# A two-layer hybrid backbone: elementwise work of the RWKV and LRU stage taken off GpSimd, and a quota on the products issued beside it

## The chip, the cores and the metric

The kernel runs on one core of a Trainium2 chip. The metric is device time in microseconds (us), the median of repeated runs. The engines are named as in the profile: PE is TensorE (PEld its weight loads), DVE is VectorE, ACT is ScalarE, POOL is GpSimd, SP is SyncE, which here issues most DMAs.

## The reference, cut to what matters

256 latent and 256 context tokens of width 1024 pass through two layers. Each layer is a half-step SwiGLU, three parallel mixers on one input projection, gated merge and output projection, and a second half-step SwiGLU. In the second layer the context tokens only feed the latent ones.

```python
z = _modulate(x, norm_g[l, 1], m[3], m[4]) @ w_in[l]          # and zc for the context tokens
ya = windowed attention(za); yl = _lru_mixer(zl, ...); yr = _rwkv_mixer(zr, ...)
# LRU, each of 2 directions: a = exp(log_a); b = sqrt(-expm1(2 log_a)) * (i * u); scan h = a h + b
# RWKV, each of 2 directions and 8 heads of 64, token by token:
sa = einsum('bhvk,bhk->bhv', s, -kk_t)
s  = s * w_t + sa * (kk_t * a_t) + v_t * k_t                  # outer products over v, k
o  = einsum('bhvk,bhk->bhv', s, r_t)
out = (g0 * (ya @ proj[0]) + g1 * (yl @ proj[1]) + g2 * (yr @ proj[2])) @ w_o   # g = sigmoid(zg)
```

## The kernel before, in words

All large matrices are multiplied in three products of a high and a low part (hi x hi, hi x lo, lo x hi). `wload` (L191 to L216) fetches a weight tile by a DMA on SP's queue, copies it to its high part on ACT (L206) and takes the difference as its low part on DVE (L215). Here the profile's phases matter: in the phases `r0` and `r1` (`POOL_PART`, L35) a quarter of the columns, 256 of 1024, is taken by POOL (L214) and DVE takes 768.

The stage that the change touches runs once per layer, between attention and the merge. It holds the LRU mixer (`lru`), the RWKV mixer (`rwkv`) and, beside them, the projections that depend on neither: 32 tiles of 24 products each, 768 products, in the generator `tiles` (8 tiles `x`, `u` feed the LRU, 24 are the gates). In the first layer a product is 512 columns wide; in the second one only the four `x` tiles are, the others are 256 wide. After the step `switch` two of the three branch projections join the queue, 192 products more.

The order of the instructions in this stage is fixed by a planner, `Weave`, when the program is built. Each mixer is split into generators (`first`, `second`, `setup`, `head`, `direction`, `pairs`, `bonus`, `decay`, `invert`, `values`, `recur`, `last`), and each `yield step(...)` announces what the next instructions will cost PE, DVE, ACT and POOL and what they need. `run` keeps a planned time `t`; it takes the step of the lowest priority number that is ready, and it issues a product instead where no step is ready, where the step at hand has PE work and the planned PE activity of the last stretch is `low`, or where an LRU tile is wanted. So the planner issues products as soon as it has a use for them, until there are none.

The RWKV recurrence is done in chunks of 64 tokens for two heads at a time (f = 0 to 3). Per f: `head` and `direction` prepare decays and keys, `pairs` multiplies them, `invert` solves a triangular system by 28 small DVE instructions between block transposes (L1160 to L1172), `invert_rest` finishes it with small matmuls (`pq`, `pw`, `pz`), `values` and `recur` carry the state (`pu`, `pM`, `po`). In the LRU, L870, L893 and L906 are POOL multiplies and adds; in RWKV POOL does L1049, L1087, L1098 and the multiply of `decay`, L1133. With DVE they form chains: ACT's tanh, POOL's product, DVE's product, and so on.

Of the kernel before, what the change touches and what calls it, by code (L numbers as in the profile page):

```python
# [26 lines left out]
NCH = T // CH  # L27
HOP, BACKLOG, WINDOW, ACTIVE, PERIOD = 0.25, 1.5, 3.4, 3.3, 50.0
E05 = float(np.exp(np.float32(-0.5)))
# [4 lines left out]
POOL_LO = {'z0': 1, 'z1': 1}  # L34
POOL_PART = {'r0': 0.25, 'r1': 0.25}  # L35
FIRST_AT = {5: [2], 6: [3, 0], 7: [1, 4]}
# [59 lines left out]
def build(tc, a, out, upto=99, dbg=None):  # L96
# [3 lines left out]
    with es:  # L100
# [472 lines left out]
        def seg3(ap):  # L573
            return ap.rearrange("p (s t) -> p s t", s=2)
# [152 lines left out]
        def step(pe=0.0, area=0.0, dve=0.0, act=0.0, pool=0.0, lag=1, need=()):  # L727


            return pe, area, (dve, act, pool), lag, need  # L730

        class Weave:
# [12 lines left out]

            def products(self):
                if not self.fill(1):
                    return False
                self.busy(*self.product)
                return True  # L750
# [7 lines left out]
            def run(self, *parts):  # L758

                at = [[b, g, None, []] for b, g in parts]  # L760
                for p in at:
                    self.advance(p, 0.0)
                while at:
                    best, soonest, wanted = None, 1e9, False
                    for p in at:
                        pe, area, eng, lag, need = p[2]
                        if any(k not in self.done for k in need):
                            wanted |= any(k[0] in "xu" for k in need)
                            continue
                        ready = p[3][-lag] if 0 < lag <= len(p[3]) else 0.0  # L770
                        ready = max([ready] + [f - BACKLOG for f, e in zip(self.free, eng) if e] + [self.done[k] for k in need])
                        soonest = min(soonest, ready)
                        if ready <= self.t and (best is None or p[0] < best[0]):
                            best = p
                    low = sum(b for a, b in self.recent if a > self.t - WINDOW) < ACTIVE
                    if best is None or (low and best[2][0]) or (wanted and self.t > self.owed):
                        if self.products():
                            self.owed = self.t + self.product[0]
                            continue
                        if best is None:  # L780
                            self.t = soonest
                            continue
                    pe, area, eng, lag, need = best[2]
                    self.busy(pe, area)
                    end = self.t
                    for i, e in enumerate(eng):
                        if e:
                            self.free[i] = max(self.free[i], self.t + HOP) + e
                            end = max(end, self.free[i] + HOP)
                    best[3].append(end)  # L790
                    best[0] += max(pe, *eng)
                    self.advance(best, end)
                    if best[2] is None:
                        at.remove(best)

            owed = 0.0

# [3 lines left out]
        def lru(l, yd, done):  # L801
# [8 lines left out]
            def first(set_):  # L810
# [30 lines left out]
                for f in range(4):  # L841
# [3 lines left out]
                    gl = lp.tile([P, T], F32, tag="gl", name=f"gl{l}{f}")  # L845
                    yield step(dve=2.1, act=0.65, need=[("x", f)] + [("scanned", f - 2)] * (f > 1))
                    ps = tile_of["x", f]
# [9 lines left out]
                    for d in range(2):  # L857
# [9 lines left out]
                        c = slice(d * 4 + f, d * 4 + f + 1)  # L867
                        yield step(dve=0.7, act=1.95, pool=1.6)
                        nc.scalar.activation(tg[1], tg[1], AF.Identity, bias=one)
                        nc.gpsimd.tensor_tensor(bb[:, d], tg[1], xc, ALU.mult)  # L870
                        nc.scalar.activation(aa[:, d], tg[0], AF.Exp, bias=n4[:, c], scale=n4[:, c])
                        nc.scalar.activation(th[:, d], tg[0], AF.Tanh, bias=n2[:, c], scale=n2[:, c])
                        nc.vector.scalar_tensor_tensor(bb[:, d], aa[:, d], 1.0, bb[:, d], ALU.add, ALU.mult)
                    yield step(dve=1.4, act=1.3, pool=0.7, need=[("u", f)])
                    ps = tile_of["u", f]
                    read[0] += 1
                    u, w, o = ps[:, qc:], gl[:, qc:], lp.tile([P, T], F32, tag="gu", name=f"gu{l}{f}", bufs=1)
                    nc.scalar.square(w, u)
                    nc.gpsimd.tensor_scalar(w, w, 0.044715, 1.0, ALU.mult, ALU.add)
                    nc.vector.tensor_tensor(w, w, u, ALU.mult)  # L880
# [5 lines left out]
            def second(set_):  # L886
                for f in range(4):
# [3 lines left out]
                    for d in range(2):  # L891
                        yield step(pool=1.6, lag=1 - d)
                        nc.gpsimd.tensor_tensor(bb[:, d], th[:, d], bb[:, d], ALU.mult)  # L893
                    for d in range(2):
                        yield step(dve=1.3, lag=2)
                        A, B, H = aa[:, d], bb[:, d], th[:, d]
                        if d == 0:
                            nc.vector.tensor_tensor_scan(H, A, B, 0.0, ALU.mult, ALU.add)
                        else:
# [3 lines left out]
                                                         H[:, 0:1], ALU.mult, ALU.add)  # L903
                    yield step(dve=0.7, pool=1.6)
                    y = lp.tile([P, T], F32, tag="yl", name=f"yl{l}{f}", bufs=1)
                    nc.gpsimd.tensor_tensor(y[:, qc:], th[:, 0, qc:], th[:, 1, qc:], ALU.add)  # L906
                    nc.vector.scalar_tensor_tensor(y[:, qc:], y[:, qc:], 0.25, gl[:, qc:], ALU.mult, ALU.mult)
# [39 lines left out]
        def step_view(ap, d):  # L947
            v = seg3(ap)
            return v if d == 0 else v[:, :, ::-1]

        def rwkv(l, rk, z, zd, yd, weave, beside, before_last):
# [7 lines left out]
            with ExitStack() as ey:  # L959
# [3 lines left out]
                wup, aup = (rx.tile([P, T], F32, tag=n, name=f"{n}{l}") for n in ("wup", "aup"))  # L963
                hv = rx.tile([P, 28], F32, tag="hv28", name=f"hv{l}")
                st, Y = {}, {}

                def setup():
# [6 lines left out]
                    nc.vector.tensor_scalar(hv[:, 20:24], V[:, R_KA:R_KA + 4], 0.5, None, ALU.mult)  # L974
                    nc.vector.tensor_scalar(hv[:, 24:28], hv[:, 20:24], -1.0, 1.0, ALU.mult, ALU.add)
                    nc.scalar.activation(twd, twd, AF.Tanh)
                    nc.scalar.activation(sgd[:, qc:], sgd[:, qc:], AF.Tanh, scale=0.5)
# [3 lines left out]
                    for f in range(4):  # L981
# [4 lines left out]
                        head_rows(pss, sq, f, 0, lambda q: f == 0, f == 3)  # L986
                    yield step(dve=4.5, act=0.4)
                    st["rsK"] = head_rsqrt(rx, rt, "tw0", pss, 0, 1.0, 1e-24, ALU.max, f"k{l}")
# [54 lines left out]
                def direction(f, d):  # L1043
                    nm = f"{l}{f}"

                    yield step(dve=1.22, pool=0.62, lag=0, need=[("tw", f)])
                    ar, bt, pc, kk, bon, tws, tas = st[f]
                    tw = tws[d]
                    nc.gpsimd.tensor_scalar(tw, tw, -0.5 * E05, -0.5 * E05, ALU.mult, ALU.add)  # L1049
                    twj = tw.rearrange("p (j t) -> p j t", t=CH)  # L1050
# [17 lines left out]
                    nc.vector.tensor_tensor(bt[:, 0, d, :, 1], ta.rearrange("p (j t) -> p j t", t=CH), iP, ALU.mult)  # L1068
                    yield step(dve=1.4, pool=1.6 * d, lag=0, need=[("one", f)] * d + [("loaded", f)] * (f > 1))
                    kks = step_view(kk, d).rearrange("p s (j t) -> p s j t", t=CH)  # L1070
# [10 lines left out]
                    if d == 0:  # L1081

                        bon.append(km)
                        weave.set("one", f)
                    else:
                        bon = bon[0]
                        nc.gpsimd.tensor_tensor(seg3(bon)[:, s0:], seg3(bon)[:, s0:], step_view(km, 1)[:, s0:], ALU.add)  # L1087
                        weave.set("both", f)
# [3 lines left out]
                def bonus(f):  # L1092

                    nm = f"{l}{f}"
                    yield step(dve=0.75, pool=1.15, lag=0, need=[("both", f)])
                    bon = st[f][4][0]

                    nc.gpsimd.tensor_copy(seg3(k_[f]), step_view(v_[f], 1))  # L1098
                    weave.set("values", f)
# [27 lines left out]
                def decay(f, d):  # L1127

                    nm = f"{l}{f}"
                    yield step(pool=1.9, lag=0, need=[("paired", f, d)])  # L1130
                    bt, pc = st[f][1:3]
                    bkT = bt[:, 0].rearrange("p d j h c -> p d j (h c)")
                    nc.gpsimd.tensor_tensor(bkT[:, d], bkT[:, d], pc[:, d, :, None].to_broadcast([P, NCH, P]), ALU.mult)  # L1133
                    for j4 in range(2):
# [248 lines left out]
                def finish(fs, pool):  # L1383

                    yield step(dve=4.5, act=0.4)
                    rsO = head_rsqrt(pool, pool, "hvo", Y["oss"], qc // P, 1.0 / 64, 64e-5, ALU.add, f"o{l}{fs[0]}")
# [257 lines left out]
```

## Time and profile before

| | |
|---|---|
| median of 3 runs | 2797.81 us (2794.79 to 2802.01) |
| the profiled execution | 2800.25 us |
| its span, first to last instruction | 2798.4 us |
| mean granted PE clock | 0.940 |
| PE, DVE, ACT, POOL busy | 94%, 62%, 38%, 15% of the span |

The stage described above lies from about 611 to 1062 us for the first layer and from about 2105 to 2560 us for the second. Busy time is the union of an engine's instructions. The granted clock is the mean over a stretch of the two levels, 1.2 GHz (0.5) and 2.4 GHz (1.0), so 0.75 means that half the stretch was at the lower one. A wait is put down to the instruction that came last. "issue" is time in which an engine waited for nothing that the profile shows.

### The profile page before, as it was taken

Reading aid. Unit: us, or ns where it says so; the run is one execution under the profiler, and the core shown is the slowest. Engines: PE = TensorE matmul, PEld = TensorE weight load, DVE = VectorE, ACT = ScalarE, POOL = GpSimd, SP = SyncE. Lnnn points to the kernel's source line nnn. Section 1 sums busy time; section 2 is a strip of 40 time slices with the busy share of each in tenths; the row PEclk is TensorE's granted clock in tenths of the full one; section 3 lists DMA queues with packets and bytes.
Section 4 is the critical chain, followed back from the end, with each engine's and each line's share of the span. In section 5 each row is a group of like instructions: output and inputs, shape, how many; then the busy total and the mean of one; then the engine's idle time right before and its main releaser. Section 6 shows DMA issues by size and latency. Waiting matters only on the chain. (4 is left out here: it accounts for less than half of the span.)

```text
span 2798.4 us, 47830 instructions
## 1 busy us (share of the span) xinstructions
PE 2629.1 (94%) x19761; PEld 2186.4 (78%) x19761; DVE 1730.3 (62%) x2934; ACT 1058.6 (38%) x1673; POOL 406.7 (15%) x381
## 2 busy tenths in 40 slices
PE   7999999997999999899999999999998899887899
PEld 5788888765677776798888978888776788777899
DVE  5867557657666644766655674555657656646565
ACT  4323233335544432332323432324346544333343
POOL 1000002224311102300000100001134432113000
PEclk9999999998898979999999999999999897768999
DMA  7646433122221125735443464544224331026465
GB/s 268 211 151 188 139 98 110 57 80 68 65 65 41 52 82 181 243 91 151 145 119 97 153 194 155 170 153 119 74 78 126 86 90 53 4 78 179 125 184 159
DMA packets 480092, 341.85 MB, mean 122 GB/s; under 512 B 17307, under 2 KB 448884, under 8 KB 479618
## 3 DMA queue, kind: packets, MB, share of 16 engines
q1 hardware_dynamic: 460690, 314.22, 37.2%
q10 hardware_dynamic: 19120, 24.52, 3.0%
q8 instruction: 155, 2.54, 0.4%
q14 instruction: 63, 0.52, 0.1%
q0 software_dynamic: 64, 0.05, 0.0%
HBM read 318.56 MB, written 20.19 MB: 121 GB/s over the span
## 5 line engine op out<-in xcount | busy, mean ns | idle before, releaser
L206 ACT CAST wh<-wr 128x1024 fp32r<-128x1024 f32 (+2 forms) x434 | 436.3, 1008 | 1079.0 <-PE gu L222 360.0
L215 DVE TENSOR_TENSOR wl<-wr,wh 128x1024 fp32r<-128x1024 f32 (+3 forms) x404 | 462.8, 1147 | 307.2 <-ACT wh L206 292.1
L222 PE MATMUL gu<-h_hi,wh 128*128 128x512 f32 (+1 forms) x1528 | 535.7, 352 | 6.2 <-ACT h_hi L388 2.6
L222 PE MATMUL gu<-h_hi,wl 128*128 128x512 f32 (+1 forms) x1528 | 534.0, 350 | 1.8 <-DVE wl L215 1.8
L222 PE MATMUL gu<-h_lo,wh 128*128 128x512 f32 (+1 forms) x1528 | 534.3, 350 | 0.7 <-DVE h_lo L389 0.5
L222 PE MATMUL win<-h_hi,wl 128*128 128x512 f32 (+1 forms) x896 | 335.0, 374 | 16.6 <-DVE wl L215 16.6
L222 PE MATMUL win<-h_hi,wh 128*128 128x512 f32 (+1 forms) x896 | 334.5, 374 | 1.1 <-ACT wh L206 0.6
L222 PE MATMUL win<-h_lo,wh 128*128 128x512 f32 (+1 forms) x896 | 332.6, 371 | 0.0
L222 PEld LDWEIGHTS gu<-h_hi,wh 128*128 128x128 f32 x1528 | 290.7, 191 | 49.8 <-ACT wh L206 6.3
L222 PEld LDWEIGHTS gu<-h_hi,wl 128*128 128x128 f32 x1528 | 291.4, 191 | 40.1 <-DVE wl L215 3.3
L222 PEld LDWEIGHTS gu<-h_lo,wh 128*128 128x128 f32 x1528 | 291.3, 191 | 37.5 <-DVE h_lo L389 1.5
L280 DVE SCALAR_TENSOR_TENSOR adacc<-adw,sc,adacc 128x1024 f32<-128x1024 f32 x196 | 245.1, 1286 | 6.0 <-ACT adacc L278 2.7
L222 PEld LDWEIGHTS win<-h_hi,wl 128*128 128x128 f32 x896 | 181.1, 202 | 57.4 <-issue 19.5
L222 PEld LDWEIGHTS win<-h_lo,wh 128*128 128x128 f32 x896 | 180.9, 202 | 36.6 <-issue 16.4
L222 PEld LDWEIGHTS win<-h_hi,wh 128*128 128x128 f32 x896 | 181.7, 203 | 32.6 <-issue 11.8
L222 PE MATMUL dn<-gh,wh 128*128 128x512 f32 (+1 forms) x560 | 200.8, 359 | 0.0
L222 PE MATMUL dn<-gl,wh 128*128 128x512 f32 (+1 forms) x560 | 199.4, 356 | 0.1
L222 PE MATMUL dn<-gh,wl 128*128 128x512 f32 (+1 forms) x560 | 199.4, 356 | 0.0
L214 POOL TENSOR_TENSOR wl<-wr,wh 128x256 fp32r<-128x256 f32 (+1 forms) x88 | 91.4, 1039 | 331.9 <-ACT wh L206 244.8
L290 POOL MEMSET adrow<- 128x256 f32 x18 | 5.6, 313 | 840.2 <-PE adt L297 840.2
L471 DVE SCALAR_TENSOR_TENSOR x<-dn,cf,x 128x256 f32<-128x256 f32 x120 | 53.6, 480 | 113.1 <-PE dn L222 112.8
L505 DVE TENSOR_TENSOR th<-th,gu 128x512 f32<-128x512 f32 (+1 forms) x88 | 54.4, 619 | 110.6 <-PE gu L222 110.4
(557 smaller groups left out, 4449.6 us busy)
## 6 DMA issues: line engine op xcount, KB each, us to landing
wr<-ffn_w_gu SPq DMA_DIRECT2D x176, 512.0 KB
adw<-ada_w SPq DMA_DIRECT2D x144, 512.0 KB
wr<-w_in SPq DMA_DIRECT2D x106, 512.0 KB
wr<-ffn_w_d SPq DMA_DIRECT2D x64, 512.0 KB
wr<-ffn_w_d SPq DMA_DIRECT2D x35, 384.0 KB
wr<-w_out SPq DMA_DIRECT2D x17, 512.0 KB
gd<-gt SPq DMA_DIRECT2D x24, 256.0 KB
wr<-branch_proj SPq DMA_DIRECT2D x24, 256.0 KB
```

Source lines behind the costliest of these rows:

```text
L206: nc.scalar.copy(hi[:, 0:w], raw[:, 0:w])
L214: nc.gpsimd.tensor_tensor(lo[:, m:w], raw[:, m:w], hi[:, m:w].bitcast(F32), ALU.subtract)
L215: eng.tensor_tensor(lo[:, 0:m], raw[:, 0:m], hi[:, 0:m].bitcast(F32), ALU.subtract)
L222: nc.tensor.matmul(ps[:, c0:c1], wt[:, k], xt(k)[:, c0:c1], start=(k == 0 and j == 0), stop=(k == kt - 1 and j == 2))
L280: nc.vector.scalar_tensor_tensor(acc, w, f, acc, ALU.mult, ALU.add)
L290: nc.gpsimd.memset(row, 0.0)
L471: nc.vector.scalar_tensor_tensor(x[:, k, cs], ps[:, cs], coef[:, s, k:k + 1], x[:, k, cs], ALU.mult, ALU.add)
L505: nc.vector.tensor_tensor(th[:, c0:], th[:, c0:], pp[1][:, c0:], ALU.mult)
```

## The change

GpSimd's elementwise work in the stage goes to other engines. To DVE: all of the low part of the weights (`POOL_PART` is empty), the LRU's three multiplies and adds (L870 fused with ACT's +1 of L869, which is gone; L893; L906), and RWKV's sum over the directions (L1087). To ACT: the scaling of the decay (L1049, now a step of its own), the copy of L1098, the polynomial of the GeLU (L879), and the multiply of `decay`, L1133, as eight instructions of 128 columns instead of one of 1024. GpSimd keeps clears, and the sum of branches in L1477. Planned costs are changed to match, `HOP` from 0.25 to 0.3, and the square roots' planned DVE cost from 4.5 to 6.5.

The planner gets a quota: a product that isn't wanted by the LRU is refused while more than 960 x (0.08 + steps taken / 390) have been issued. A refused product leaves the step at hand to be issued, or the planned time to move on.

```diff
-POOL_PART = {'r0': 0.25, 'r1': 0.25}
+STEPS, PRODUCTS, AHEAD = 390, 960, 0.08
+POOL_PART = {}
...
-            def products(self):
+            def products(self, wanted=False):
+                if not wanted and self.sent > PRODUCTS * (AHEAD + self.steps / STEPS):
+                    return False
                 if not self.fill(1):
                     return False
+                self.sent += 1
...
-                        if self.products():
+                        if self.products(wanted):
...
                     pe, area, eng, lag, need = best[2]
+                    self.steps += 1
...
-                        yield step(dve=0.7, act=1.95, pool=1.6)
-                        nc.scalar.activation(tg[1], tg[1], AF.Identity, bias=one)
-                        nc.gpsimd.tensor_tensor(bb[:, d], tg[1], xc, ALU.mult)
+                        yield step(dve=1.4, act=1.3)
+                        nc.vector.scalar_tensor_tensor(bb[:, d], tg[1], 1.0, xc, ALU.add, ALU.mult)
...
-                    nc.gpsimd.tensor_scalar(w, w, 0.044715, 1.0, ALU.mult, ALU.add)
+                    nc.scalar.activation(w, w, AF.Identity, bias=one, scale=0.044715)
...
-                        yield step(pool=1.6, lag=1 - d)
-                        nc.gpsimd.tensor_tensor(bb[:, d], th[:, d], bb[:, d], ALU.mult)
-                    for d in range(2):
-                        yield step(dve=1.3, lag=2)
+                        yield step(dve=2.0, lag=1 - d)
+                        nc.vector.tensor_tensor(bb[:, d], th[:, d], bb[:, d], ALU.mult)
...
-                    nc.gpsimd.tensor_tensor(y[:, qc:], th[:, 0, qc:], th[:, 1, qc:], ALU.add)
+                    nc.vector.tensor_tensor(y[:, qc:], th[:, 0, qc:], th[:, 1, qc:], ALU.add)
...
-                    yield step(dve=1.22, pool=0.62, lag=0, need=[("tw", f)])
-                    nc.gpsimd.tensor_scalar(tw, tw, -0.5 * E05, -0.5 * E05, ALU.mult, ALU.add)
+                    yield step(act=0.63, lag=0, need=[("tw", f)])
+                    nc.scalar.activation(tw, tw, AF.Identity, bias=hv[:, 28:29], scale=-0.5 * E05)
+                    yield step(dve=1.22)
...
-                        nc.gpsimd.tensor_tensor(seg3(bon)[:, s0:], seg3(bon)[:, s0:], step_view(km, 1)[:, s0:], ALU.add)
+                        nc.vector.tensor_tensor(seg3(bon)[:, s0:], seg3(bon)[:, s0:], step_view(km, 1)[:, s0:], ALU.add)
...
-                    nc.gpsimd.tensor_copy(seg3(k_[f]), step_view(v_[f], 1))
+                    nc.scalar.copy(seg3(k_[f]), step_view(v_[f], 1))
...
-                    yield step(pool=1.9, lag=0, need=[("paired", f, d)])
-                    nc.gpsimd.tensor_tensor(bkT[:, d], bkT[:, d], pc[:, d, :, None].to_broadcast([P, NCH, P]), ALU.mult)
+                    yield step(act=2.0, lag=0, need=[("paired", f, d)])
+                    for j in range(NCH):
+                        nc.scalar.activation(bkT[:, d, j], bkT[:, d, j], AF.Copy, scale=pc[:, d, j:j + 1])
```

## Rows read from the trace of the kernel before

**Rows 1.** Busy time by stretch (us): PE, PEld, DVE, ACT, POOL (instructions); then granted clock.

```profile
611.00:740.00 129.00, 108.28 (x593) 76.50 (x594) 95.59 (x177) 66.72 (x95) 47.64 (x43) 0.88 0.27 76
740.00:1062.00 322.00, 319.27 (x4112) 242.44 (x4111) 183.03 (x340) 134.79 (x217) 59.72 (x55) 0.90 0.21 63
2105.00:2240.00 135.00, 112.20 (x780) 90.83 (x780) 97.73 (x174) 83.18 (x119) 58.58 (x57) 0.89 0.38 108
2240.00:2338.00 98.00, 93.40 (x1306) 81.10 (x1305) 61.93 (x107) 45.00 (x77) 27.15 (x28) 0.89 0.31 91
2338.00:2465.00 127.00, 103.69 (x1917) 90.13 (x1915) 79.42 (x169) 47.82 (x86) 18.80 (x17) 0.73 0.03 8
```

**Rows 2.** The same view for instructions on the tiles of products (`win`) alone.

```profile
620.00:740.00 120.00, 68.58 (x260) 50.33 (x260) 14.49 (x20) 7.29 (x11) 0.87 0.27 75
2105.00:2240.00 135.00, 87.06 (x497) 75.15 (x497) 12.91 (x22) 9.52 (x21) 0.89 0.38 108
2240.00:2338.00 98.00, 45.11 (x275) 38.78 (x273) 0.00 (x0) 4.56 (x12) 0.89 0.31 91
2338.00:2465.00 127.00, 0.00 (x0) 0.00 (x0) 0.00 (x0) 0.00 (x0) 0.73 0.03 8
```

**Rows 3.** Waits of PE from 2340 to 2480: total us, times, longest.

```profile
PE pq L1187 <- DVE XZ L1172: 12.0, 2, 6.0
PE pz L1218 <- DVE XZ L1207: 8.2, 3, 3.2
```

**Rows 4.** Waits of PE from 2100 to 2340.

```profile
PE win L222 <- DVE wl L215: 16.0, 6, 5.1
```

**Rows 5.** Busy time on the tile `pz`, by stretch: PE, PEld, ACT; clock.

```profile
2235.00:2340.00 105.00, 4.50 (x128) 4.16 (x128) 2.31 (x4) 0.89 0.32 94
2340.00:2480.00 140.00, 20.53 (x384) 20.13 (x384) 6.92 (x12) 0.70 0.05 15
```

**Rows 6.** The same on the tile `pu`.

```profile
2235.00:2340.00 105.00, 5.24 (x64) 4.12 (x64) 4.63 (x8) 0.89 0.32 94
2340.00:2480.00 140.00, 14.71 (x128) 13.11 (x128) 9.26 (x16) 0.70 0.05 15
```

**Rows 7.** Chain of waits, from 2090 to 2580: start, us, what.

```profile
2160.17 3.52 POOL km L1087
...
2175.39 2.54 POOL bb L893 x2
...
2200.51 0.92 POOL gl L879
...
2251.57 3.79 PE win L222 x30
```

**Rows 8.** Groups of DVE instructions by form, 612 to 1062: count, busy us, mean ns.

```profile
L215 DVE TENSOR_TENSOR wl<-wr,wh 128x768 fp32r<-128x768 f32 x32 | 34.9, 1090 | 33.1 <-ACT wh L206 21.9 <-issue 9.2 <-ACT W L1273 1.8
L898 DVE TENSOR_TENSOR_SCAN th<-aa,bb 128x512 f32<-128x512 f32 x4 | 8.1, 2018 | 6.3 <-POOL bb L893 6.3
L873 DVE SCALAR_TENSOR_TENSOR bb<-aa,bb 128x512 f32<-128x512 f32 x8 | 5.5, 691 | 16.8 <-POOL bb L870 13.6 <-ACT th L872 3.1
```

**Rows 9.** The same view over the whole span.

```profile
L215 DVE TENSOR_TENSOR wl<-wr,wh 128x1024 fp32r<-128x1024 f32 x273 | 335.8, 1231 | 218.9 <-ACT wh L206 218.2
```

**Rows 10.** DVE in order of time: start, us.

```profile
2207.47 0.18 DVE L1167 TENSOR_TENSOR XZ<-XZ 64x28 f32<-64x28 f32 x1
2207.69 1.40 DVE L1169 TENSOR_TENSOR XZ<-XZ 64x28 f32<-64x28 f32 x1
...
2215.60 1.21 DVE L898 TENSOR_TENSOR_SCAN th<-aa,bb 128x512 f32<-128x512 f32 x1
```

**Rows 11.** Groups of ACT instructions by form, 612 to 1062.

```profile
L1139 ACT COPY bt<-pk 128x512 f32<-128x512 f32 x16 | 9.1, 587 | 38.4 <-PE pk L1138 34.0 <-POOL wl L214 2.3 <-POOL XZ L1162 2.0
L869 ACT ACTIVATE tg<-tg,ones 128x512 f32<-128x512 f32 x8 | 5.8, 720 | 0.0
L1286 ACT COPY ar<-pM 128x192 f32<-128x192 f32 x8 | 2.5, 319 | 4.8 <-PE pM L1284 4.8
```

More of the change, by code (lines that the diff above doesn't have):

```diff
@@ L27 @@
 NCH = T // CH
-HOP, BACKLOG, WINDOW, ACTIVE, PERIOD = 0.25, 1.5, 3.4, 3.3, 50.0
+HOP, BACKLOG, WINDOW, ACTIVE, PERIOD = 0.3, 1.5, 3.4, 3.3, 50.0
+STEPS, PRODUCTS, AHEAD = 390, 960, 0.08
 E05 = float(np.exp(np.float32(-0.5)))
@@ L794, in run @@
                         at.remove(best)
-            owed = 0.0
+            owed, sent, steps = 0.0, 0, 0
         tile_of, read = {}, [0]
@@ L845, in first @@
                     gl = lp.tile([P, T], F32, tag="gl", name=f"gl{l}{f}")
-                    yield step(dve=2.1, act=0.65, need=[("x", f)] + [("scanned", f - 2)] * (f > 1))
+                    yield step(dve=2.3, act=0.65, need=[("x", f)] + [("scanned", f - 2)] * (f > 1))
                     ps = tile_of["x", f]
@@ L873, in first @@
                         nc.vector.scalar_tensor_tensor(bb[:, d], aa[:, d], 1.0, bb[:, d], ALU.add, ALU.mult)
-                    yield step(dve=1.4, act=1.3, pool=0.7, need=[("u", f)])
+                    yield step(dve=1.4, act=2.0, need=[("u", f)])
                     ps = tile_of["u", f]
@@ L903, in second @@
                                                          H[:, 0:1], ALU.mult, ALU.add)
-                    yield step(dve=0.7, pool=1.6)
+                    yield step(dve=1.4, lag=0)
                     y = lp.tile([P, T], F32, tag="yl", name=f"yl{l}{f}", bufs=1)
-                    nc.gpsimd.tensor_tensor(y[:, qc:], th[:, 0, qc:], th[:, 1, qc:], ALU.add)
+                    nc.vector.tensor_tensor(y[:, qc:], th[:, 0, qc:], th[:, 1, qc:], ALU.add)
                     nc.vector.scalar_tensor_tensor(y[:, qc:], y[:, qc:], 0.25, gl[:, qc:], ALU.mult, ALU.mult)
@@ L963, in rwkv @@
                 wup, aup = (rx.tile([P, T], F32, tag=n, name=f"{n}{l}") for n in ("wup", "aup"))
-                hv = rx.tile([P, 28], F32, tag="hv28", name=f"hv{l}")
+                hv = rx.tile([P, 29], F32, tag="hv29", name=f"hv{l}")
                 st, Y = {}, {}
@@ L975, in setup @@
                     nc.vector.tensor_scalar(hv[:, 24:28], hv[:, 20:24], -1.0, 1.0, ALU.mult, ALU.add)
+                    nc.vector.memset(hv[:, 28:29], -0.5 * E05)
                     nc.scalar.activation(twd, twd, AF.Tanh)
@@ L986, in setup @@
                         head_rows(pss, sq, f, 0, lambda q: f == 0, f == 3)
-                    yield step(dve=4.5, act=0.4)
+                    yield step(dve=6.5, act=0.4)
                     st["rsK"] = head_rsqrt(rx, rt, "tw0", pss, 0, 1.0, 1e-24, ALU.max, f"k{l}")
@@ L1068, in direction @@
                     nc.vector.tensor_tensor(bt[:, 0, d, :, 1], ta.rearrange("p (j t) -> p j t", t=CH), iP, ALU.mult)
-                    yield step(dve=1.4, pool=1.6 * d, lag=0, need=[("one", f)] * d + [("loaded", f)] * (f > 1))
+                    yield step(dve=1.4 + 0.7 * d, lag=0, need=[("one", f)] * d + [("loaded", f)] * (f > 1))
                     kks = step_view(kk, d).rearrange("p s (j t) -> p s j t", t=CH)
@@ L1094, in bonus @@
                     nm = f"{l}{f}"
-                    yield step(dve=0.75, pool=1.15, lag=0, need=[("both", f)])
+                    yield step(dve=0.75, act=0.6, lag=0, need=[("both", f)])
                     bon = st[f][4][0]
-                    nc.gpsimd.tensor_copy(seg3(k_[f]), step_view(v_[f], 1))
+                    nc.scalar.copy(seg3(k_[f]), step_view(v_[f], 1))
                     weave.set("values", f)
@@ L1383, in finish @@
                 def finish(fs, pool):
-                    yield step(dve=4.5, act=0.4)
+                    yield step(dve=6.5, act=0.4)
                     rsO = head_rsqrt(pool, pool, "hvo", Y["oss"], qc // P, 1.0 / 64, 64e-5, ALU.add, f"o{l}{fs[0]}")
```

## The prediction

> **What bounds the kernel now.** I read the span in 40 slices first: PE is at 9 in almost every slice, and its granted clock sags in the second half of the second layer. Then busy time by stretch over the two stages of mixers [rows 1]. In the first layer the lead-in, 611 to 740 us, has PE busy 108.3 of 129.0, and after that 319.3 of 322.0 with a clock of 0.90: PE sets the pace there. In the second layer the lead-in is 112.2 of 135.0, the middle 93.4 of 98.0, and from 2338 to 2465 PE works 103.7 of 127.0 at a clock of 0.73, which means that 54% of that stretch is at 1.2 GHz instead of 2.4.
>
> The count of products says why [rows 2]: of the second layer's 768 products (and 4 of the stage ahead) 497 lie before 2240, 275 before 2338 and none after it. The planner has spent them. From there PE waits for DVE's inversion, 12.0 us for `pq` and 8.2 us for `pz` [rows 3], and the small matmuls run slowly: `pz` took 4.50 us for one f while products lay beside it and 20.53 us for three later [rows 5], `pu` 5.24 us for one and 14.71 us for two [rows 6]. Conversely, in the early part products arrive faster than their weights: PE waited 16.0 us for low parts [rows 4]. The chain of waits shows what else binds the lead-in: between 2160 and 2201 us nine pieces of POOL, 0.7 to 3.5 us each, 14.1 us together [rows 7].
>
> **The quota.** After the change a layer's stage has 395 steps (first layer) or 387 (second): 49 of the LRU, 11 of `setup` and `outputs`, 80 or 78 for each f, and 15 others. The quota grows by 960/390 = 2.46 products a step from 77.
>
> In the first layer 768 products over 395 steps are 1.94 a step, and at 740 us, some 100 steps in, 260 have gone [rows 2] where 77 + 246 = 323 are allowed. It hardly binds; I cost it at nothing there, with ±4 us for the order that it, `HOP` and the new step costs shuffle.
>
> In the second layer it binds. Counted from which yields had been issued, 2240 us is about step 104 and 2338 about step 186. The quota allows 333 and 535 products by then, where 497 and 772 were issued. So 164 leave the first stretch, 73 more the second, and about 233 land behind it, until the quota reaches 768 at step (0.8 - 0.08) x 390 = 281 (about the inversion of f = 2). One product takes 3.79 / 30 = 0.126 us [rows 7].
> - Lead-in: 164 x 0.126 = 20.7 us less PE work. PE was idle 22.8 us there, so it isn't the bound throughout; the ends are 0 and -20.7, and I take half, -10. What is late next is DVE's and ACT's chain of the LRU.
> - Middle: 73 x 0.126 = 9.2 us, with PE busy 95%: I take -9, ends -3 and -9.2.
> - Behind: 233 x 0.126 = 29.4 us are added. The waits for the inversion, 20.2 us [rows 3], hide at most that; the last f's inversion comes after the products, so I take 15 hidden and 14 on the path. The clock returns 20.53 - 3 x 4.50 = 7.0 us on `pz` and 14.71 - 2 x 5.24 = 4.2 us on `pu`, 11.2 together; I take 10 of it, and leave the other forms for the range. That is +4, with ends of -10 and +24.
>
> The quota's sum is -15 us. The weight DMAs and ACT's high parts move with their products; SP only waits for buffers, and a slower stream of tiles gives DVE more time for each low part, so the 16.0 us is part of the lead-in's gain and not counted again.
>
> **POOL's work on DVE and ACT.** DVE gains per layer three groups of the LRU and one of RWKV: 8 + 8 + 4 + 4 instructions at 0.691 us (L873, the same form and size [rows 8]) = 16.6 us in the first layer, about 14 in the second, where two of the groups are half as wide. Its low parts go from 768 to 1024 columns, 1.090 to 1.231 us [rows 8, 9]: 32 x 0.14 = 4.5 us. Sum 21 and 19 us. It loses what POOL cost it: a DVE instruction of 28 columns took 0.18 us and the like of it next took 1.40 [rows 10], and the scan L898 took 2.018 us on average [rows 8] against 1.21 in a quiet place [rows 10], 4 x 0.8 = 3.2 us per layer from this line alone.
>
> The Trainium skill's page "SBUF — State Buffer" (section "SBUF: two separate sides") says that GpSimd and a DVE instruction with two SBUF inputs share one pair of ports by an exclusive lock held for the whole instruction. Rows 10 agree. By that rule moving work between the two adds next to nothing to DVE, and the first layer's term below would be -16 instead of -8, the total 2758.
>
> ACT gains L1049 and L879, 8 + 4 at 0.720 us, L1098 4 at 0.587, and `decay`, 64 instructions of 128 columns. From 0.587 us at 512 and 0.319 at 192 columns [rows 11] the slope is 0.84 ns, so 0.265 us at 128, 17 us (20 at most, by 0.319). L869 goes, -5.8. Net 22 us on an engine busy 45% of these stretches [rows 1], and eight pieces take 2.1 us where POOL took 1.9. What queues behind them on ACT are copies out of PSUM for PE, later by 2 us at most, 16 times in the kernel; products or the next steps lie beside that. I cost it at 0, with +6 if that cover is gone.
>
> On the path, the nine POOL pieces of the second layer's chain (14.1 us) become about 5: three products, two more and a sum on DVE at 0.4 to 0.69 us, two longer low parts at 0.14, one ACT piece. That is -9 us, ends 0 and -14. The first layer's lead-in has the same chains, PE idle 20.7 of 129 us, DVE busy 74%. I take -8 there, nearer to the second layer's row than to the ends of -16 and +19 (all added DVE work on the path). Behind 740 us PE has no idle time to give: 0.
>
> **Sum.** -10 - 9 + 4 - 9 - 8 = -32 us from the profiled 2800.25, and from the median, 2.4 us lower, 2797.8 - 32 = 2766.
>
> **Rivals.**
> - *More of it.* Both early terms in full (-20.7, -9.2), the late products hidden by all 20.2 us and the clock back (+9.2 - 11.2), the chain -14 and the first layer -16: -62, 2736. For it: the waits and the low clock are real and adjacent. Against: the products end before the last f.
> - *The clock falls early.* With a third fewer products the lead-in and the middle could drop to the 0.73 that the starved stretch shows: from 22% to 54% at 1.2 GHz, over 205.6 us of PE work 66 us more. In 2340 to 2480, 84 us at that level cost at least 11.2 us, 0.13 per us; all work in proportion would be 0.5. That is +9 to +33; I take +16, total -16, 2782. Against: in the first layer a clock of 0.87 to 0.90 held with 1.94 products a step. Those were twice as wide, however, which speaks for it. The skill's page "TensorE: Matmul & The Clock Gate" (Part 1) says that the low clock is the default and activity lifts it. The granted 0.73 after the products end agrees.
> - *Products only change places.* What the early stretches lose comes back in the late one, its 29.4 us unhidden but for the waits' half (10) and with no clock returned: -10 - 9 + 19 = 0 for the quota, and of the -17 from POOL's work two thirds, as the lead-ins then wait elsewhere: -11, 2787. For it: the chain through DVE's inversion is no shorter.
> - *DVE becomes the bound (slower).* All the added DVE work, 21 + 19 us, lies on the path, without relief and without the chain's gain; the quota's -15 remains: +25, 2823. It decides once DVE is busy over about 95% of the lead-ins. They stand at 74% and 72% [rows 1]; the LRU's share of the additions takes them to about 88%. The wait of PE for low parts would grow beyond 16.0 us.
>
> **How the numbers follow.** Forecast 0.45 (its own range 2748 to 2785), more of it 0.18, clock 0.17, places 0.11, DVE 0.09. The range 2733 to 2798 reaches into the cases on both sides and leaves the slower one out. About 0.3%, 8 us, is what a measurement of this kernel can tell from no change. Faster by more: the first two whole, most of the third, half of the fourth, 0.83. Within: 0.08. Slower: 0.09.
>
> **What would show it.** In the second layer's stage, products should lie in each stretch up to about the inversion of f = 2, with some 330 rather than 497 before the place where the LRU ends. The granted clock behind should rise from 0.73 to over 0.8, `pz` to some 5 us for one f, the wait of `pq` for the inversion should halve and that of products for low parts nearly vanish. POOL should be under 20 us in each stage, and short DVE instructions should lose their stretches of 1.2 to 1.4 us. Wrong would be: a lower clock before 2240, a PE waiting more for DVE in either lead-in, or a late stretch that grows by the whole 29 us.

## The result, and the profile after

The changed kernel takes 2769.52 us (2764.53 to 2771.72, 4 runs) against 2798.64 us: ratio 0.9894, 95% interval 0.9875 to 0.9913. The forecast was 2766. The total came out; its parts did not, as the experiments show.

The page of the changed kernel, span and busy time:

```profile
span 2769.9 us, 47656 instructions
PE 2621.5 (95%) x19761; PEld 2178.9 (79%) x19761; DVE 1732.8 (63%) x2984; ACT 1107.9 (40%) x1817; POOL 191.3 (7%) x197
```

I measure a layer's stage from its first small DVE instruction to the last branch product (first layer) or the first output product (second). From the instructions' start times, the first layer goes from 521.2 to 496.7 us, -24.5, and the second from 448.1 to 440.2, -7.9. The forecast had -8 and -24; some 4 us of the stages' gain went elsewhere. The product count of the first lead-in [rows 2] rises, at a clock of 0.97 instead of 0.87, to this (columns as there):

```profile
620.00:740.00 120.00, 86.14 (x328) 61.56 (x327) 15.68 (x22) 9.09 (x14) 0.97 0.32 90
```

Within the second layer the matmuls `pq`, one group per f, are milestones. PE in order of time, before (start, us, idle before):

```profile
2235.53 2.20 PE L1187 MATMUL pq<-XZ,bt 16*32 16x16 f32 x128
2324.74 2.20 PE L1187 MATMUL pq<-XZ,bt 16*32 16x16 f32 x128
2391.39 3.59 PE L1187 MATMUL pq<-XZ,bt 16*32 16x16 f32 x128 [6.01 <-DVE XZ L1172]
2453.93 3.59 PE L1187 MATMUL pq<-XZ,bt 16*32 16x16 f32 x128 [6.01 <-DVE XZ L1172]
```

and after:

```profile
2199.00 3.21 PE L1193 MATMUL pq<-XZ,bt 16*32 16x16 f32 x128
2279.38 2.20 PE L1193 MATMUL pq<-XZ,bt 16*32 16x16 f32 x128
2357.71 2.20 PE L1193 MATMUL pq<-XZ,bt 16*32 16x16 f32 x128
2429.46 3.60 PE L1193 MATMUL pq<-XZ,bt 16*32 16x16 f32 x128 [7.70 <-DVE XZ L1178]
```

From the stage's start (2108.1 and 2089.9) they stand at 127, 217, 283, 346 before and at 109, 189, 268, 340 after: -18, -27, -15, -6. The early gain is there and the late part gives three quarters of it back. Products lie in it as planned (busy time on `win` after, as in rows 2):

```profile
2087.00:2199.00 112.00, 59.55 (x336) 49.72 (x335) 12.10 (x20) 7.03 (x14) 0.88 0.32 90
2199.00:2279.00 80.00, 30.34 (x187) 24.37 (x186) 0.84 (x2) 3.09 (x8) 0.91 0.27 76
2279.00:2358.00 79.00, 33.69 (x198) 27.28 (x198) 0.00 (x0) 3.43 (x9) 0.87 0.25 74
2358.00:2430.00 72.00, 10.79 (x47) 8.21 (x47) 0.00 (x0) 0.77 (x2) 0.77 0.10 32
```

but the small matmuls beside them stay slow: for f = 1 and 2 `pz` took 6.21 and 6.28 us, where [rows 5] gave 4.50 us beside products and 20.53 / 3 = 6.84 without them. `pu` took 7.62 and 7.09 us, where [rows 6] gave 5.24 and 14.71 / 2 = 7.36. The tile `pz`, then `pu`, after:

```profile
2280.00:2358.00 78.00, 6.21 (x128) 5.72 (x128) 2.31 (x4) 0.87 0.24 71
2358.00:2430.00 72.00, 6.28 (x128) 5.76 (x128) 2.31 (x4) 0.77 0.10 32
```

```profile
2280.00:2358.00 78.00, 7.62 (x64) 6.43 (x64) 4.64 (x8) 0.87 0.24 71
2358.00:2430.00 72.00, 7.09 (x64) 6.69 (x64) 4.64 (x8) 0.77 0.10 32
```

### The profile page after: what moved, and what is told of

The parts are those of the page before. It is cut to its first block, busy times and chain, and to the rows that moved or that the text cites. A ratio compares the mean times of both kernels' runs of the same rounds, so it can differ in the third digit from the quotient of the medians.

```text
span 2769.9 us, 47656 instructions
## 1 busy us (share of the span) xinstructions
PE 2621.5 (95%) x19761; PEld 2178.9 (79%) x19761; DVE 1732.8 (63%) x2984; ACT 1107.9 (40%) x1817; POOL 191.3 (7%) x197
## 5 line engine op out<-in xcount | busy, mean ns | idle before, releaser
L216 DVE TENSOR_TENSOR wl<-wr,wh 128x1024 fp32r<-128x1024 f32 (+2 forms) x404 | 474.1, 1175 | 291.2 <-ACT wh L207 287.1
L223 PEld LDWEIGHTS dn<-gh,wh 128*128 128x128 f32 x560 | 105.2, 188 | 16.9 <-ACT wh L207 1.3
L223 PEld LDWEIGHTS dn<-gh,wl 128*128 128x128 f32 x560 | 105.0, 188 | 16.5
```

Of the source, the lines that this page charges most:

```text
L216: eng.tensor_tensor(lo[:, 0:m], raw[:, 0:m], hi[:, 0:m].bitcast(F32), ALU.subtract)
L223: nc.tensor.matmul(ps[:, c0:c1], wt[:, k], xt(k)[:, c0:c1], start=(k == 0 and j == 0), stop=(k == kt - 1 and j == 2))
```

## The experiments

**The change taken apart.** Kernel by kernel, each timed beside the kernel before.

`quota_only`: the kernel before with the quota's lines of the diff alone. 

> Before, with the quota alone (960 x (0.08 + steps / 390)); all engines and planned costs as before. The prediction's theory: the quota binds in the second layer only and is worth -15 us there; 2783. The rival, formed from the two traces: the quota saves in the lead-in what the late stretch gives back, since the late products are only partly hidden and the clock of pz and pu does not return; within 5 us of no change, 2793 to 2803. Both: first layer within 4 us.


Measured 2798.45 us, ratio 1.001 (0.9989 to 1.003): nothing. Its milestones show the loan and its repayment; from its start at 2105.9 they are 113, 205, 283, 345:

```profile
2218.95 2.20 PE L1192 MATMUL pq<-XZ,bt 16*32 16x16 f32 x128
2311.03 2.20 PE L1192 MATMUL pq<-XZ,bt 16*32 16x16 f32 x128
2389.30 2.20 PE L1192 MATMUL pq<-XZ,bt 16*32 16x16 f32 x128
2450.82 3.59 PE L1192 MATMUL pq<-XZ,bt 16*32 16x16 f32 x128 [6.01 <-DVE XZ L1177]
```

It is 14 us ahead at f = 0, 12 at f = 1 and 0 at f = 2, though the wait of `pq` went there (the one at f = 3 stayed). The low clock moved with the products. Busy time on `pz` and the clock between these milestones (columns as in rows 5):

```profile
2106.00:2219.00 113.00, 0.00 (x0) 0.00 (x0) 0.00 (x0) 0.83 0.30 80
2219.00:2311.00 92.00, 7.65 (x128) 7.11 (x128) 2.31 (x4) 0.87 0.24 69
2311.00:2389.00 78.00, 7.30 (x128) 6.77 (x128) 2.31 (x4) 0.80 0.23 66
2389.00:2451.00 62.00, 4.41 (x128) 4.19 (x128) 2.21 (x4) 0.89 0.16 47
```

`pz` of f = 2 took 4.41 us here instead of 6.84, as at the high clock, but that of f = 0 took 7.65 instead of 4.50, and the lead-in stands at 0.83 instead of 0.89. Over the whole second stage the mean clock is 0.83, against 0.82 before.

`moves_only`: the changed kernel, with
```diff
-                if not wanted and self.sent > PRODUCTS * (AHEAD + self.steps / STEPS):
+                if not wanted and self.sent > 10 ** 6:
```


> After, with a quota that never refuses. The prediction's theory: -17 us (chain of the second layer -9, first layer -8), 2781. The rival: the moves and their planned costs make the first layer 24 us shorter and the second some 8, so this kernel is as fast as the changed one or within 5 us of it, 2765 to 2775; the second layer's products run out before the inversion of f = 1 again.


2761.03 us, 0.9851 (0.981 to 0.9893): not slower than with the quota, whose interval, 0.9875 to 0.9913, overlaps. It lies 4 us below the rival's range and 20 below the prediction's 2781, and `pq` waits for the inversion of f = 1 again, as the rival has it. The first two milestones, from a start at 2088.2:

```profile
2219.54 2.20 PE L1193 MATMUL pq<-XZ,bt 16*32 16x16 f32 x128
2296.61 3.54 PE L1193 MATMUL pq<-XZ,bt 16*32 16x16 f32 x126 [6.61 <-DVE XZ L1178]
```

They stand at 131 and 208, so without the quota the moves are 4 us behind the kernel before at f = 0 and 8 us ahead at f = 1.

`old_plan`: `moves_only`, with the planner's numbers and steps of before, for instance
```diff
-HOP, BACKLOG, WINDOW, ACTIVE, PERIOD = 0.3, 1.5, 3.4, 3.3, 50.0
+HOP, BACKLOG, WINDOW, ACTIVE, PERIOD = 0.25, 1.5, 3.4, 3.3, 50.0
...
-                    yield step(act=2.0, lag=0, need=[("paired", f, d)])
+                    yield step(pool=1.9, lag=0, need=[("paired", f, d)])
                     for j in range(NCH):
                         nc.scalar.activation(bkT[:, d, j], ...)
```


> After without quota, and with the step costs, HOP and steps of before in the planner: the new engines under the old plan. If the first layer's 24 us come from the engines (shorter chains from ACT to DVE, no GpSimd in DVE's way), most remains: first layer -15 or more, whole 2770 to 2785. If they come from the plan (longer planned waits, so 71 more products before 740 us), the first layer gains under 8 us: 2785 to 2800.


2747.8 us, 0.9824 (0.9804 to 0.9844): better than the kernel before and the changed one. Stages 499.2 and 422.8, -22 and -25. The engines make the whole gain, and it is larger than the first theory's range (2770 to 2785). The plan theory is out.

`new_plan`: the kernel before, with the changed planner's numbers and steps, the reverse of the diff above. 

> Before without quota, with the step costs, HOP and steps of the changed kernel in the planner: the old engines under the new plan. Engines: no gain, 2793 to 2810, since POOL's work is then planned on DVE and ACT and POOL's own queue is not planned at all. Plan: the first layer takes more products into its lead-in and gains 12 us or more, 2770 to 2786.


2802.52 us, 1.0026 (1.0008 to 1.0043); stages 511.4 and 464.1, -10 and +16. The plan moves time from one layer to the other and gains none.

**What about the engines.** Each kernel here is `old_plan` with one thing changed.

`pool_low`, `POOL_PART` back:
```diff
-POOL_PART = {}
+POOL_PART = {'r0': 0.25, 'r1': 0.25}
```


> The new engines under the old plan (2748 us), with a quarter of each low part back on GpSimd (37 us of its time per layer). If the gain is that chains are shorter, this matters where products wait for low parts: +5, 2750 to 2757. If it is that GpSimd no longer holds up DVE, this part has the largest share of GpSimd's time, about 37 of 100 us, and so of the 47 us: +17, 2760 to 2770.


2764.19 us, 0.9901 (0.9862 to 0.9941).

`pool_lru`, the LRU's lines back:
```diff
-                        nc.vector.scalar_tensor_tensor(bb[:, d], tg[1], 1.0, xc, ALU.add, ALU.mult)
+                        nc.scalar.activation(tg[1], tg[1], AF.Identity, bias=one)
+                        nc.gpsimd.tensor_tensor(bb[:, d], tg[1], xc, ALU.mult)
...
```


> The new engines under the old plan, with the LRU's work back on GpSimd and ACT (L870, L879, L893, L906 of before; 31 us of GpSimd per layer). Chains: the lead-ins hang on the LRU, +20 to +30, 2768 to 2778. GpSimd in DVE's way: its share, +15, 2758 to 2768.


2762.51 us, 0.9887 (0.9851 to 0.9922).

`pool_rwkv`, RWKV's back:
```diff
-                    for j in range(NCH):
-                        nc.scalar.activation(bkT[:, d, j], bkT[:, d, j], AF.Copy, scale=pc[:, d, j:j + 1])
+                    nc.gpsimd.tensor_tensor(bkT[:, d], bkT[:, d], pc[:, d, :, None].to_broadcast([P, NCH, P]), ALU.mult)
...
```


> The new engines under the old plan, with RWKV's work back on GpSimd (L1049, L1087, L1098, L1133 of before; 32 us per layer). Chains: the recurrence waits for decay only once per f and direction and products cover it, +5 to +10, 2753 to 2760. GpSimd in DVE's way: its share, +15, 2758 to 2768.


2760.44 us, 0.988 (0.9849 to 0.9911). The three cost 16, 15 and 13 us over `old_plan`'s 2748, or 22, 18 and 16 us if each ratio to the kernel before is set against `old_plan`'s 0.9824. Together that is 44 to 55 us, where the gain was 47 to 49. In the two stages GpSimd is busy for 98, 67 and 66 us longer. All three times lie in the ranges of the theory that GpSimd holds up DVE, and none in those of the chains. But the intervals, of about 10 us to either side, reach into both and can't rank the three, so this alone doesn't decide.

`pool_idle_work`:
```diff
+            if phase[0][:1] == "r":
+                for _ in range(6):
+                    nc.gpsimd.tensor_tensor(selT[:, 4], selT[:, 4].bitcast(F32), selT[:, 4].bitcast(F32), ALU.mult)
```


> The new engines under the old plan, and beside each weight tile of the two stages six multiplies of 128 columns on GpSimd that nobody reads or waits for (a table of zeros and ones times itself; some 80 us per layer, where 100 were removed). Chains: nothing is behind them but clears, 0 to +6, 2745 to 2755. GpSimd in DVE's way: most of the gain is lost again, +20 to +40, 2768 to 2788.


2881.92 us, 1.0322, and no answer: waiting for nothing, the work ran ahead of the stage, in the attention stage, and delayed the low parts there. Groups of POOL by form, 430 to 700 us of this kernel, and PE's longest wait in that time (total us, times, longest):

```profile
L215 POOL TENSOR_TENSOR selT<-selT 128x128 fp32r<-128x128 f32 x288 | 116.4, 404 | 23.4 <-PE hba L568 1.5
L219 POOL TENSOR_TENSOR wl<-wr,wh 128x1024 fp32r<-128x1024 f32 x15 | 35.6, 2373 | 70.1 <-ACT wh L207 70.1
PE win L226 <- POOL wl L219: 59.4, 8, 10.1
```

`pool_spent_tiles`, the same question with the work tied to its place:
```diff
+            if phase[0][:1] == "r" and w == 1024:
+                for h in (raw[:, 0:512], raw[:, 512:1024]):
+                    nc.gpsimd.tensor_tensor(h, h, h, ALU.mult)
```


> The new engines under the old plan (2748 us), and behind each 1024-wide weight tile of the two stages two multiplies of 512 columns on GpSimd, in place on the fetched tile after its last reader: some 80 us of GpSimd per layer that nothing reads; only the DMA three tiles later waits for it. GpSimd in DVE's way: it costs what the three undone parts cost per us of GpSimd, 44 us for 100, so +35, 2775 to 2790. Chains: no consumer is behind it, 0 to +6, 2745 to 2755.


2778.29 us, 0.9947 (0.9923 to 0.997), 30 us over `old_plan` (34 by the two ratios): in the first theory's range and far above the chains'. DVE's work is the same in both. Busy time over the two stages (PE, PEld, DVE, ACT, POOL; then the granted clock), `old_plan`:

```profile
620.70:1119.90 499.20, 477.11 (x4946) 357.40 (x4945) 317.17 (x604) 244.72 (x413) 26.60 (x29) 0.94 0.31 90
2079.10:2501.90 422.80, 366.99 (x4708) 314.26 (x4707) 284.22 (x576) 228.47 (x402) 18.87 (x31) 0.85 0.29 84
```

`pool_spent_tiles`:

```profile
622.70:1127.70 505.00, 478.85 (x4946) 358.56 (x4945) 335.83 (x604) 244.94 (x413) 98.57 (x95) 0.93 0.30 89
2097.60:2536.50 438.90, 372.27 (x4682) 318.39 (x4682) 314.42 (x577) 227.89 (x401) 117.38 (x108) 0.83 0.28 80
```

and the kernel before:

```profile
624.90:1146.10 521.20, 490.57 (x4944) 366.54 (x4943) 317.16 (x578) 219.13 (x341) 134.08 (x127) 0.91 0.29 86
2108.10:2556.20 448.10, 380.81 (x4708) 326.03 (x4707) 284.06 (x551) 204.02 (x330) 124.56 (x122) 0.82 0.27 79
```

170 us more of GpSimd make the same DVE work 49 us longer. And from before to `old_plan` DVE takes over some 40 us of work and is busy for 601.2 and 601.4 us: what it took over, it had been losing. The instructions that are the same in both show it directly: 1029 of them, by form and tiles, add up to 546 us before and 505 in `old_plan` (558 in `pool_spent_tiles`).

One reservation: in `pool_spent_tiles` SP also waited for the spent tiles, in the first stage and in the second:

```profile
SPq L201 <- POOL wr L219: 72.4, 31, 3.3
SPq L201 <- POOL wr L219: 90.8, 38, 9.5
```

In the second stage PE's waits of products for weights (`wl` and `wh`) grow from 10.4 to 19.7 us, more than half of that stage's 16 us. How much of the 30 us comes from later weights and how much from a slower DVE isn't separated. It isn't separated for the gain either: of the 47 us in the stages from before to `old_plan`, 27 are PE's own busy time, for nearly the same matmuls at a clock of 0.94 and 0.85 instead of 0.91 and 0.82, and 20 are idle time of PE.

**Could it be better still?** `quota_first`, `old_plan` with the quota in the first layer only:
```diff
-                if not wanted and self.sent > 10 ** 6:
+                if not wanted and self.product[0] > 0.2 and self.sent > PRODUCTS * (AHEAD + self.steps / STEPS):
```


> The new engines under the old plan, with the quota in the first layer alone. The first layer was 4.7 us shorter with the quota in both pairs that had it (before against the quota alone, and the changed kernel without and with it), the second layer is left as it is: 2743, within 2738 to 2748. Theory that those 4.7 us were chance between two profiles: no change, 2748.


2747.27 us, 0.9829 (0.9806 to 0.9853): no change.

`hop_and_sqrt`, `old_plan` with
```diff
-HOP, BACKLOG, WINDOW, ACTIVE, PERIOD = 0.25, 1.5, 3.4, 3.3, 50.0
+HOP, BACKLOG, WINDOW, ACTIVE, PERIOD = 0.3, 1.5, 3.4, 3.3, 50.0
...
-                    yield step(dve=4.5, act=0.4)
+                    yield step(dve=6.5, act=0.4)
... (and the same in `finish`)
```


> The new engines under the old plan, with two of the changed planning numbers: HOP 0.3 and 6.5 for the square roots' DVE time. All new planning numbers together cost 13 us. If the longer planned waits draw products forward into the second layer's lead-in, these two do most of it: 2755 to 2763. If it is the steps without GpSimd's time, nothing: 2745 to 2751.


2737.62 us, 0.9799 (0.9773 to 0.9824): not slower, and its interval overlaps `old_plan`'s. These two numbers are not what costs 13 us in the new plan, if anything does; its other steps were not tried.

`no_pool_attention`, `old_plan` with
```diff
-POOL_LO = {'z0': 1, 'z1': 1}
+POOL_LO = {}
```


> The new engines under the old plan, and in the attention stage too all low parts on DVE (half of them were on GpSimd, 2.4 us each). GpSimd in DVE's way: DVE is busy 117 of 190 us there beside 38 us of GpSimd; in proportion 0.44 per us of GpSimd over 71 us in both layers, -15 to -30, 2718 to 2733. Chains: PE is busy 181 of 190 us and the low part comes half as late; -5 to 0, 2743 to 2748. DVE as the bound: 32 low parts at 1.23 us more on it, +5 to +15.


2725.44 us, 0.9744 (0.9719 to 0.977), the fastest of all, 22 us below `old_plan`. That is within the first theory's range, but the range came from a wrong rate: 0.44 sets the 44 us of both layers against GpSimd's 100 us of one. Over both it is 0.22, so 71 us would be 16. The attention stage, PE first, in `old_plan` and then here:

```profile
430.00:621.00 191.00, 182.47 (x1041) 142.83 (x1040) 118.24 (x297) 65.93 (x148) 38.24 (x19) 0.97 0.26 78
```

```profile
430.00:621.00 191.00, 189.17 (x1093) 148.85 (x1092) 127.98 (x353) 73.05 (x159) 2.44 (x5) 1.00 0.31 88
```

PE waited there for no low part of GpSimd, so the chains theory's shorter way to the low part isn't the gain. Its longest wait in `old_plan` was for DVE, and here it is gone:

```profile
PE py L696 <- DVE pT L687: 5.1, 3, 1.8
```

DVE instructions of two columns show what GpSimd's low parts cost DVE; by form, `old_plan` (430 to 620) and then here:

```profile
L665 DVE SCALAR_TENSOR_TENSOR mx<-mx,sk 128x2 f32<-128x2 f32 x16 | 7.7, 481 | 0.4
```

```profile
L665 DVE SCALAR_TENSOR_TENSOR mx<-mx,sk 128x2 f32<-128x2 f32 x16 | 2.5, 156 | 0.2
```

## Why the prediction came out, and what in it was wrong

The number is right by luck: two terms were wrong by similar amounts in opposite directions. The quota was forecast at -15 us and gave none, and the moves were forecast at -17 and gave twice to almost three times that (-34 in `moves_only`, -47 in `old_plan`).

- *The early terms of the quota* (-10 and -9) with the chain's -9 make -28 to the inversion of f = 1, and -27 was measured. The count was right too: 333 and 535 products allowed, 336 and 523 issued at the two milestones. The split was not. The quota's whole early gain lies before f = 0, 14 us alone and 22 beside the moves (the changed kernel against `moves_only`). Of the middle's -9 it gave nothing: at f = 1 its lead is 12 and 19 us. The middle became shorter by the moves, which had no term there, and the lead-in's -9 for the chain isn't to be seen in `moves_only`, 4 us behind at f = 0 (it is with the old steps: `old_plan` is 16 us ahead there).
- *The late term* (+4) failed. From f = 1 to f = 3 the changed kernel takes 150.1 us where 129.2 were taken: +21. One step that failed is the price of a product, 0.126 us, taken from one piece of the chain [rows 7]; the middle stretch of [rows 2] has 45.11 / 275 = 0.164. The 245 products that now lie there (20 before) kept PE busy for 44.5 us, 0.17 and 0.23 us each, at clocks of 0.87 and 0.77. The other is "The clock returns", priced at 10 us: `pz` gave back 1.2 us for f = 1 and 2, `pu` nothing. The wait before `pq` did vanish for f = 2 and stayed, with 7.70 us, for f = 3. So the quota's -15 is 0 alone, and beside the moves not a gain either (0.9894 with it, 0.9851 without). That is the rival "products only change places", for this part.
- *The clock falls early*, another rival, wasn't seen in the changed kernel, with 0.88 and 0.91 up to f = 1 against 0.89 and 0.89 [rows 1]. It was in `quota_only`, with 0.83 and 0.87.
- *The moves' term* (-9 and -8) was far too small: the engines alone are worth -47, -22 and -25 by stage. The step that failed is that only GpSimd's pieces on one chain were priced (14.1 us to 5), and its hold on DVE elsewhere by a single line, "4 x 0.8 = 3.2 us per layer from this line alone", set against 21 and 19 us of added DVE work. The stages' DVE time shows relief of the whole 40 us. The rule of the Trainium skill's page "SBUF — State Buffer" (section "SBUF: two separate sides"), weighed in the prediction as adding "next to nothing to DVE", agrees with these 601.2 against 601.4 us. How much of the 47 us came through this relief and how much through shorter chains stays open.
- *The first layer* got -24.5 instead of -8, of which the moves make about 20 (some 502 us in `moves_only`). That the quota hardly binds there held: `quota_first` changes nothing.
- *ACT's cost at 0* was not tried alone. A piece of `decay` took 390 ns instead of 265, so its eight pieces take 3.1 us where 2.1 were counted.
- *DVE as the bound*, the slower rival, has nothing for it: DVE was busy for 601.2 us in the two stages before and for 604.0 in the changed kernel.

The new step costs, which the prediction priced at ±4 us, may cost more with the new engines, 13 us by the medians of `moves_only` and `old_plan`. Their intervals overlap (0.981 to 0.9893 and 0.9804 to 0.9844), so this isn't shown.

## What to carry to other kernels

Price a GpSimd elementwise instruction as DVE time too: where both are in use, moving it to DVE can be free. Here the kernel became faster by a fifth to a third of the GpSimd time that was taken away (47 us for some 210, 22 us for 71). GpSimd work that nobody reads cost 30 us for 170, later weights included. Filler work that is postponed from one stretch to another is paid there, at that stretch's clock, unless the engine idles for as long as the filler takes; a wait that disappears isn't yet a gain. Check the sum of a forecast part by part: a right total can hide two wrong terms. When a change has several parts, time each alone: here one part gained 47 us, and with the other two the whole gained 29.

## What was not expected of the hardware

A two-column DVE instruction took 481 ns on average beside GpSimd and 156 ns without it. In the changed kernel the clock did not come back for the small matmuls by laying 198 products between the milestones: `pz` stayed at 6.2 us, with a mean granted clock of 0.87 over that stretch. In `quota_only` it came back for `pz` of f = 2, with 4.41 us beside 67 products, and was lost for that of f = 0, with 7.65: the low clock moved, and the stage's mean stayed at 0.82 to 0.83.
